# Down and output projections by token, with rows of the weights moving

## Chip, cores, metric

The kernel runs on one core of a Trainium2 chip. The metric is the time of one execution on the device, in microseconds (us).

## What is computed

A trunk of two layers over 256 tokens with 1024 channels, all in float32. Each layer is a gated ffn, a mixer and a second ffn; a norm stands ahead of each and behind the last.

```
def reference(x, ...):
    for l in range(L):
        h = rms_norm(x, ffn1_norm[l])
        x = x + 0.5 * swiglu_ffn(h, w_gate, w_up, w_down)   # 1024 -> 2816 -> 1024
        h = rms_norm(x, mix_norm[l])
        a_val, a_gate, b_u, b_v, c_b, c_c, c_x = split(h @ w_in[l])   # 1024 -> 2432
        a = a_val * sigmoid(a_gate)
        a = causal_depthwise_conv(a, conv_a_w[l]) + conv_a_b[l]       # 31 taps
        a = silu(layer_norm(a, ln_a_g[l], ln_a_b[l]))
        b = chunked_spatial_gating(gelu(b_u), gelu(b_v), ...)
        c = c_b * causal_depthwise_conv(c_c * c_x, conv_c_w[l])       # 3 taps
        x = x + concat(a, b, c) @ w_out[l]                            # 1024 -> 1024
        h = rms_norm(x, ffn2_norm[l])
        x = x + 0.5 * swiglu_ffn(h, ...)
    return rms_norm(x, final_norm)
```

## The kernel before, in words

The residual `x_sb` lies by channel: 8 tiles `x[d]` of 128 channels by 256 tokens. Weights come as float32 pages of 128x1024 (`load_to`, L114, six buffers). `split_to` (L121) divides a page into a high part `hi`, a cast on ACT (L128), and a low part `lo`, a difference on VectorE (L129), up to 14 pages ahead of their use. Activations are split in the same way and lie side by side as [high, low], 512 columns. `mm` (L170) is the product that fills nearly all of the time: a block of the high weights stands in the array and 512 columns move (L175), then the block of the low weights and 256 columns (L176). Here the two are called a pair. `whole` (L178) adds the two halves of the result with a copy on ACT and a sum on VectorE. Where float32 is used without a split, `mm_native` (L147) gives native products, which run as two instructions each; in the profile all of them have line L149.

An ffn (L349) goes through 22 hidden tiles in two halves of 11. For each tile it has 8 pairs for gate (`f_pg`) and 8 for up (`f_pu`); the results are multiplied on VectorE and ACT and split (`f_m`). Then the down projection of the half follows, `f_pd`, 8 output tiles of 11 pairs, each added to `x[d]`. In the second half `Norm.feed` (L297) makes the next stage's activations from each `x[d]` at once: scaled by the norm's gain and split. The norm's factor, which depends on the token alone, is applied later, to the results. Its sums over the channels are products with a column of ones (`token_sums`, L266), its inverse root a chain of small steps on VectorE (`rsqrt_rows`, L236), and it is spread to all partitions by products of 128x128 with an identity (L260). The first tile of the first ffn is native, because no page is split yet.

The mixer (L463 on) has 19 output tiles of 8 pairs in the combined projection (`m_p`). Group A runs a convolution over VectorE and ACT and then a layer norm (`m_la`, L412), on which the last three inputs of the output projection depend. Five of the eight output tiles of the output projection (`m_po`) are native, three in pairs. First come the inputs of groups B and C, and behind the layer norm those of A. The last step is the final norm and the multiply of `x_sb` by it (L669).

Order of work: each engine runs its instructions in a fixed order, which a scheduler derives from the program; where `pin` is used the program's own order stays.

Of the kernel before, what the change touches and what calls it, by code (L numbers as in the profile page):

```python
# [44 lines left out]
NCOLS = L * LCOLS + DT  # L45
# [7 lines left out]
IN_ORDER += [t for i in range(NC) for t in (C_C + i, C_X + i, C_B + i)]  # L53

PAGE_BLOCKS = 8
PAGE = PAGE_BLOCKS * P
RAWS = 6
PARTS = 15
LOAD_AHEAD = 6
AHEAD = 14  # L60
PACE = 1.6
NEXT = 4
# [14 lines left out]
def hybrid_trunk(ctx, tc, x_t, par, w_st, b_s, wts, out):  # L77
# [7 lines left out]
    ps_mm = ctx.enter_context(tc.tile_pool(name="ps_mm", bufs=6, space=PSUM))  # L85
    ps_sm = ctx.enter_context(tc.tile_pool(name="ps_sm", bufs=2, space=PSUM))

    spare = []

    def single(name):  # L90

        if not spare:
            pair = work.tile([P, 2, T], F32, tag="w", name=f"{name}_2")
            spare.extend([pair[:, 1, :], pair[:, 0, :]])
        return spare.pop()

# [14 lines left out]
    state = {"at": 0, "cap": None, "credit": 0.0}  # L111
# [20 lines left out]
    def native(n):  # L132

        at = state["at"]
        state["at"] += n
        last = (at + n - 1) // PAGE_BLOCKS
        load_to(last + LOAD_AHEAD)
        got = []
        for i in range(at, at + n):
            raw = loaded[i // PAGE_BLOCKS]  # L140
            c = i % PAGE_BLOCKS * P
            got.append(raw[:, c:c + P])
        while len(pages) <= last:
            pages.append(None)
        return got

    def mm_native(ps, w, act, ks, first, last):  # L147
        for k in ks:
            nc.tensor.matmul(ps, w[k], act[k], start=k == first, stop=k == last)  # L149

    def weights(n, ahead=True):
# [3 lines left out]
        last = (at + n - 1) // PAGE_BLOCKS  # L155
        split_to(last + 1)
        if ahead:
            state["credit"] += n * PACE / PAGE_BLOCKS
            to = min(last + 1 + AHEAD, len(pages) + int(state["credit"]))
# [3 lines left out]
        got = []  # L163
        for i in range(at, at + n):
            hi, lo = pages[i // PAGE_BLOCKS]
            c = i % PAGE_BLOCKS * P
            got.append((hi[:, c:c + P], lo[:, c:c + P]))
        return got

    def mm(ps, w, act, ks, first, last):  # L170


        for k in ks:
            (wh, wl), x2 = w[k], act[k]
            nc.tensor.matmul(ps, wh, x2, start=k == first, stop=False)  # L175
            nc.tensor.matmul(ps[:, 0, :], wl, x2[:, 0, :], start=False, stop=k == last)  # L176
# [11 lines left out]

    ones_sq = const.tile([P, P], F32, name="ones_sq")
    nc.vector.memset(ones_sq, 1.0)  # L190

    ps = ps_sm.tile([P, P], F32, tag="sm", name="warm")
    for _ in range(WARM):
        nc.tensor.matmul(ps, ones_sq, ones_sq, start=True, stop=True)
    x_sb = acts.tile([P, DT, T], F32, tag="x", name="x_sb")
    x = [x_sb[:, d, :] for d in range(DT)]
    xall = x_t.rearrange("p (d t) -> p d t", t=T)
    par_sb = const.tile([P, NCOLS], F32, name="par_sb")
    nc.sync.dma_start(par_sb, par)
    for i in range(2):  # L200
        raw = raws.tile([P, PAGE], F32, tag="raw", name=f"raw{i}")
        loaded.append(raw)
    Q, H = DT // 4, PAGE // 2
    for n, (i, h) in enumerate(((0, 0), (1, 0), (0, 1), (1, 1))):
        nc.sync.dma_start(x_sb[:, n * Q:(n + 1) * Q, :], xall[:, n * Q:(n + 1) * Q, :])
        nc.sync.dma_start(loaded[i][:, h * H:(h + 1) * H], wts[i][:, h * H:(h + 1) * H])
    ident = const.tile([P, P], F32, name="ident")
# [20 lines left out]
    def col(l, name, i):  # L228
        c = (L * LCOLS if name == "final_norm" else l * LCOLS + COL[name]) + i
# [501 lines left out]
```

## Time and profile before

| | |
|---|---|
| median of 3 runs | 962.69 us (960.36 to 965.59) |
| profiled execution | 961.55 us |
| its span, mean clock of TensorE | 959.8 us, 0.985 |
| PE (TensorE, products) | 934.6 us busy, 97% |
| PEld (its weight loads, beside PE) | 812.6 us, 85% |
| DVE (VectorE) | 776.9 us, 81% |
| ACT (ScalarE) | 568.7 us, 59% |
| DMA | 170.70 MB, 178 GB/s in the mean |

A span is the time from the first to the last instruction of one profiled execution. Shares are busy time over the span; clock is the share of full speed that TensorE had. Engines wait for each other by semaphores, and a wait is put down to what came last.

### The profile page before, as it was taken

The numbers are of one execution on the slowest core, as the hardware profiler recorded it, in microseconds if no ns is written. First come the engines' busy times: TensorE is split into PE (matmuls) and PEld (weight loads), VectorE is DVE, ScalarE is ACT, GpSimd is POOL, SyncE is SP. The second block draws the span as 40 slices with busy tenths as digits, with TensorE's granted clock in tenths as the row PEclk, the third lists the DMA queues.
The fourth block names the chain that finished last, engine by engine and source line by source line (L and its number), as shares of the span: only waits on it lengthen the run. The fifth ranks groups of instructions, "written<-read, shape, count | busy, mean of one in ns | idle before, by whom it ended". The sixth has DMA issues, their size and how long they took to land.

```text
span 959.8 us, 14578 instructions
## 1 busy us (share of the span) xinstructions
PE 934.6 (97%) x5280; PEld 812.6 (85%) x5280; DVE 776.9 (81%) x1456; ACT 568.7 (59%) x1052; POOL 3.0 (0%) x14
## 2 busy tenths in 40 slices
PE   9999999999979999999999999999997999999995
PEld 7888888888868888888888888888886888888885
DVE  6998777878969997777987777778987799878733
ACT  6875555578257864555655545556952677645522
POOL 0000000000000000000000000000000000000000
PEclk9999999999979999999999999999998999999998
DMA  8995555530037975555555555554300789555101
GB/s 297 320 347 192 185 194 188 186 133 22 17 114 261 340 272 184 190 195 181 189 181 186 187 190 186 195 184 145 111 1 0 245 284 341 196 188 194 45 1 44
DMA packets 48024, 170.70 MB, mean 178 GB/s; under 512 B 5328, under 2 KB 5712, under 8 KB 47952
## 3 DMA queue, kind: packets, MB, share of 16 engines
q1 hardware_dynamic: 47952, 169.77, 50.8%
q8 instruction: 41, 0.67, 0.3%
q14 instruction: 31, 0.25, 0.1%
HBM read 168.71 MB, written 1.05 MB: 177 GB/s over the span
## 4 chain that ended last, share of the span: by engine, by line
PE 91%; DVE 6%; DMA 2%; ACT 1%; issue 0%; DVEq 0%; SPq 0%
PE f_pd L175 17%; PE f_pu L175 17%; PE f_pg L175 17%; PE f_pd L176 9%; PE f_pu L176 8%; PE f_pg L176 8%; PE m_p L175 7%; PE m_p L176 4%; PE m_po L149 1%; DMA raw<-wts 1%; DVE m_ac_acc L458 1%; DVE lo L129 1%; DVE m_ac_acc L451 1%; PE f_pg L149 1%; DMA x_sb<-x_t 0%
## 5 line engine op out<-in xcount | busy, mean ns | idle before, releaser
L129 DVE TENSOR_TENSOR lo<-raw,hi 128x1024 fp32r<-128x1024 f32 x306 | 371.8, 1222 | 95.3 <-ACT hi L128 93.8
L128 ACT CAST hi<-raw 128x1024 fp32r<-128x1024 f32 x306 | 318.8, 1051 | 212.8 <-PE f_pd L175 71.6
L175 PE MATMUL f_pg<-ffn_norm_x,hi 128*128 128x512 f32 x696 | 247.4, 395 | 1.7 <-DVE ffn_norm_x L302 1.7
L175 PE MATMUL f_pd<-f_m,hi 128*128 128x512 f32 x704 | 247.2, 396 | 0.0
L175 PE MATMUL f_pu<-ffn_norm_x,hi 128*128 128x512 f32 x696 | 247.0, 394 | 0.0
L176 PE MATMUL f_pd<-f_m,lo 128*128 128x256 f32 x704 | 195.5, 280 | 0.0
L176 PE MATMUL f_pg<-ffn_norm_x,lo 128*128 128x256 f32 x696 | 194.4, 279 | 0.0
L176 PE MATMUL f_pu<-ffn_norm_x,lo 128*128 128x256 f32 x696 | 194.3, 279 | 0.0
L175 PEld LDWEIGHTS f_pd<-f_m,hi 128*128 128x128 f32 x704 | 131.9, 188 | 32.1 <-DVE f_m L334 1.4
L175 PEld LDWEIGHTS f_pg<-ffn_norm_x,hi 128*128 128x128 f32 x696 | 130.5, 187 | 32.3 <-DVE ffn_norm_x L302 2.3
L175 PEld LDWEIGHTS f_pu<-ffn_norm_x,hi 128*128 128x128 f32 x696 | 130.5, 187 | 30.0
L176 PEld LDWEIGHTS f_pd<-f_m,lo 128*128 128x128 f32 x704 | 132.8, 189 | 0.5
L176 PEld LDWEIGHTS f_pg<-ffn_norm_x,lo 128*128 128x128 f32 x696 | 131.2, 188 | 0.3 <-DVE lo L129 0.3
L176 PEld LDWEIGHTS f_pu<-ffn_norm_x,lo 128*128 128x128 f32 x696 | 131.2, 188 | 0.1
L175 PE MATMUL m_p<-mix_norm_x,hi 128*128 128x512 f32 x304 | 108.1, 398 | 0.0
L176 PE MATMUL m_p<-mix_norm_x,lo 128*128 128x256 f32 x304 | 85.9, 283 | 0.0
L175 PEld LDWEIGHTS m_p<-mix_norm_x,hi 128*128 128x128 f32 x304 | 57.1, 188 | 12.9
L176 PEld LDWEIGHTS m_p<-mix_norm_x,lo 128*128 128x128 f32 x304 | 57.4, 189 | 0.4 <-issue 0.2
L389 ACT ACTIVATE f_sg<-f_g 128x256 f32<-128x256 f32 x88 | 36.4, 414 | 17.5 <-DVE f_g L387 17.3
L185 DVE TENSOR_TENSOR f_wd_sm<-f_pd,f_wd_lo 128x256 f32<-128x256 f32 x64 | 26.8, 419 | 20.6 <-ACT f_wd_lo L183 20.6
L333 ACT CAST f_m<-f_m 128x256 fp32r<-128x256 f32 x88 | 35.4, 402 | 10.5 <-DVE f_m L391 7.2
L458 DVE SCALAR_TENSOR_TENSOR m_ac_acc<-apad,par_sb,m_ac_acc 128x256 f32<-128x256 f32 x90 | 40.8, 481 | 0.8 <-ACT m_ac_acc L446 0.7
(242 smaller groups left out, 843.2 us busy)
## 6 DMA issues: line engine op xcount, KB each, us to landing
raw<-wts SPq DMA_DIRECT2D x316, 512.0 KB, 4.3
x_sb<-x_t SPq DMA_DIRECT2D x4, 256.0 KB, 5.2
raw<-wts SPq DMA_DIRECT2D x4, 256.0 KB, 5.4
out<-x_sb SPq DMA_DIRECT2D x4, 256.0 KB, 2.4
wst<-w_st SPq DMA_DIRECT2D x2, 256.0 KB, 4.3
bsb<-b_s SPq DMA_DIRECT2D x2, 128.0 KB, 4.2
par_sb<-par SPq DMA_DIRECT2D x1, 143.0 KB, 2.3
```

Source lines behind the costliest of these rows:

```text
L128: nc.scalar.copy(hi, loaded[i])
L129: after(nc.vector.tensor_sub(lo, loaded[i], hi), held[0])
L149: nc.tensor.matmul(ps, w[k], act[k], start=k == first, stop=k == last)
L175: nc.tensor.matmul(ps, wh, x2, start=k == first, stop=False)
L176: nc.tensor.matmul(ps[:, 0, :], wl, x2[:, 0, :], start=False, stop=k == last)
L185: nc.vector.tensor_add(sm, ps[:, 0, :], lo)
L333: nc.scalar.copy(x2[:, 0, :], src)
L389: nc.scalar.activation(sg, g, AF.Silu)
L451: nc.vector.tensor_add(acc, acc, t)
L458: yield lambda j=j: nc.vector.scalar_tensor_tensor(acc[:, j % 4, :], ap[:, j:j + T], wt[j], acc[:, j % 4, :], ALU.mult, ALU.add)
```

## The change

The down and the output projection are turned round. The activation, a half of 128 tokens, stands in the array, and a row of a weight page moves, 512 columns at a time. The result lies by token. It takes three products (`mm_out`) for each token half c and column half h, and the four results (c, h) take four banks of PSUM that stay open through the whole stage. So the down projection of hidden tile f - 2 follows gate and up of tile f; the last three tiles are done bank by bank. `x_sb` lies by token as well: `x[c, h]`, 128 tokens by 512 channels. For the next norm each x must be turned back, by transposes on TensorE (`Norm.turn`), and the sum of squares comes from ACT as it squares (`accum_out`). The combined projection uses three products of 256 columns into one bank half, and no `whole`. In the output projection five inputs are split, all banks at once, and the three of group A are native, bank by bank. Buffers for raw pages go from 6 to 5, PSUM is 3 + 1 + 4 banks where it was 6 + 2, and pages are split up to 11 ahead, not 14. The pages of the weights are laid out in another order on the host, and x comes in two layouts.

```
+    def mm_three(ps, page, act, ks):
+        for k in ks:
+            (wh, wl), x2 = block(page, k), act[k]
+            nc.tensor.matmul(ps, wh, x2[:, 0, :], start=k == 0, stop=False)
+            nc.tensor.matmul(ps, wh, x2[:, 1, :], start=False, stop=False)
+            nc.tensor.matmul(ps, wl, x2[:, 0, :], start=False, stop=k == DT - 1)
+    def mm_out(ps, x2, page, c, h, first, last):
+        t, n = slice(c * P, (c + 1) * P), slice(h * N, (h + 1) * N)
+        if len(x2.shape) == 2:
+            nc.tensor.matmul(ps, x2[:, t], page[:, n], start=first, stop=last)
+            return
+        xh, xl = x2[:, 0, t], x2[:, 1, t]
+        wh, wl = (p[:, n] for p in page)
+        nc.tensor.matmul(ps, xh, wh, start=first, stop=False)
+        nc.tensor.matmul(ps, xh, wl, start=False, stop=False)
+        nc.tensor.matmul(ps, xl, wh, start=False, stop=last)
...
 class Norm:
+        def sums(self):
+            sq = [parts.tile([P, 4, T], F32, tag="pg", name=f"{self.id}_sq{i}") for i in range(2)]
+            for s, t in zip(sq, xt):
+                nc.scalar.activation(s, t, AF.Square)
+            s = sq[0]
+            nc.vector.tensor_add(s, s, sq[1])
+            nc.vector.tensor_add(s[:, :2, :], s[:, :2, :], s[:, 2:, :])
+            nc.vector.tensor_add(s[:, 0, :], s[:, 0, :], s[:, 1, :])
+            self.rs = rsqrt(token_sums([s[:, 0, :]], self.id), 1.0 / D, RMS_EPS, self.id)
+        def square(self, c, h):
+            sq = tmp.tile([P, N], F32, tag="sq", name=f"{self.id}_sq{c}{h}")
+            nc.scalar.activation(sq, x[c, h], AF.Square, accum_out=self.ss[:, c, h:h + 1])
+        def turn(self, c, h):
+            pt = small([P, 4, P], f"{self.id}_pt{c}{h}")
+            for d in range(4):
+                pin(nc.tensor.transpose(pt[:, d, :], x[c, h][:, d * P:(d + 1) * P], ident))
+            xg = tmp.tile([P, 4, P], F32, tag="xg", name=f"{self.id}_xg{c}{h}")
+            g = col(self.l, self.name, 4 * h, 4).rearrange("p (d o) -> p d o", o=1)
+            nc.vector.tensor_mul(xg, pt, g.broadcast_to([P, 4, P]))
+            hi, lo = (self.x2[h][:, :, i, c * P:(c + 1) * P] for i in range(2))
+            nc.scalar.copy(hi, xg)
+            nc.vector.tensor_sub(lo, xg, hi)
+        def lead(self, tiles, want):
+            ks = range(DT // 2), range(DT // 2, DT)
+            got = None
+            for mm, ps, w in tiles:
+                mm(ps, w, self.act, ks[0])
+                while self.later:
+                    self.later.pop(0)()
+            for mm, ps, w in tiles:
+                mm(ps, w, self.act, ks[1])
+                if got is None:
+                    got = self.rows(want)
+            return got
+    def drain_banks(order, bank, scale, nxt):
+        for n, (c, h) in enumerate(order):
+            ps = bank(c, h)
+            if n:
+                nxt.turn(*order[n - 1])
+            if scale is None:
+                nc.vector.tensor_add(x[c, h], ps, x[c, h])
+            else:
+                nc.vector.scalar_tensor_tensor(
+                    x[c, h], ps, scale[:, c:c + 1], x[c, h], ALU.mult, ALU.add)
+            nxt.square(c, h)
+        nxt.rstd()
+        nxt.later.append(lambda: nxt.turn(*order[-1]))
...
 def ffn(l, s, norm, nxt):
...
+            split_to(4)
+            norm.sums()
+            tiles[1] = [psum(wide, f"{nm}_1_pg")]
+            w1 = weights(2, False)
+            mm_wide(tiles[1][0], w1[0], act, range(DT))
+            rb, = norm.rows([AF.Copy])
...
+            if LAG <= f < FT - LAST + LAG:
+                for b in banks:
+                    down(f - LAG, *b)
+        def bank(c, h):
+            for f in range(FT - LAST, FT):
+                down(f, c, h)
+            return pd[c, h]
+        nxt.open()
+        if nxt.end:
+            finish(bank, rh, nxt)
+        else:
+            drain_banks(banks, bank, rh, nxt)
+    def finish(bank, scale, nxt):
+        for c in range(TC):
+            gx = []
+            for h in range(2):
+                ps = bank(c, h)
+                nc.vector.scalar_tensor_tensor(
+                    x[c, h], ps, scale[:, c:c + 1], x[c, h], ALU.mult, ALU.add)
+                nxt.square(c, h)
+                y = tmp.tile([P, N], F32, tag="xg", name=f"y{c}{h}")
+                nc.vector.tensor_mul(y, x[c, h], gfin[0][:, h * N:(h + 1) * N])
+                gx.append(y)
+            s = tmp.tile([P, 1], F32, tag="fin_s", name=f"fin_s{c}")
+            nc.vector.tensor_add(s, nxt.ss[:, c, 0:1], nxt.ss[:, c, 1:2])
+            r = rsqrt(s, 1.0 / D, RMS_EPS, f"fin{c}", 1)
+            for h, y in enumerate(gx):
...
+                nc.sync.dma_start(out[c, :, h * N:(h + 1) * N], y)
...
 def mixer(l, norm, nxt):
...
+        for k in OUT_ORDER[:DT - NA]:
+            w = weights(1, False)[0]
+            for c, h in banks:
+                mm_out(po[c, h], mix[k], w, c, h, k == first, k == last)
+        wn = dict(zip(OUT_ORDER[DT - NA:], native(NA)))
...
+        def bank(c, h):
+            for k in OUT_ORDER[DT - NA:]:
+                mm_out(po[c, h], mix[k], wn[k], c, h, k == first, k == last)
+            return po[c, h]
+        nxt.open()
+        drain_banks(banks, bank, None, nxt)
```

`mm_wide` is the old pair under a new name, pinned to the program's order.

**The start, TensorE.** Before, behind the native products of the first tile (`f_0`) the first pairs of the second tile follow, then the token sums (`ffn_norm_ps`):

```order
L149 MATMUL f_0_pu<-ffn_norm_xg_2_142,raw_94 128x256
L149 MATMUL f_0_pu<-ffn_norm_xg_2_151,raw_94 128x256 x2
L175 MATMUL f_1_pg<-ffn_norm_x_126,hi_190 128x512 [waits Activation_49]
L176 MATMUL f_1_pg<-ffn_norm_x_126,lo_191 128x256 [waits DVE_49]
L175 MATMUL f_1_pg<-ffn_norm_x_130,hi_190 128x512
L270 MATMUL ffn_norm_ps<-ones,ffn_norm_sq_200 128x1 [waits DVE_49]
L270 MATMUL ffn_norm_ps<-ones,ffn_norm_sq_200 128x1
```

In the change, where the natives have line L183 and pairs L191 and L192:

```order
L183 MATMUL f_0_pu<-ffn_norm_xg_2_146,raw_98 128x256
L183 MATMUL f_0_pu<-ffn_norm_xg_2_153,raw_98 128x256 x2
L309 MATMUL ffn_norm_ps<-ones,ffn_norm_sq_198 128x1 [waits DVE_49,PE_49]
L309 MATMUL ffn_norm_ps<-ones,ffn_norm_sq_198 128x1
L191 MATMUL f_1_pg<-ffn_norm_x_129,hi_188 128x512 [waits Activation_49]
L192 MATMUL f_1_pg<-ffn_norm_x_129,lo_189 128x256
```

The token sums now stand ahead of the first pair.

**Border from the first ffn to mixer 0, VectorE in the change.** L407 adds the four banks of the down projection (`f_pd`) to x, L365 multiplies a transposed bank (`mix_norm_pt`) by the gain, L368 is its low part, L276 to L287 are the inverse root, L152 is the low part of a page.

```order
L407 SCALAR_TENSOR_TENSOR x_sb<-f_pd_386,f_rh,x_sb 128x512 [waits PE_49]
L407 SCALAR_TENSOR_TENSOR x_sb<-f_pd_390,f_rh,x_sb 128x512 [waits PE_49]
L365 TENSOR_TENSOR mix_norm_xg_2021<-mix_norm_pt_2016,par_sb 128x512 [waits PE_49]
L407 SCALAR_TENSOR_TENSOR x_sb<-f_pd_394,f_rh,x_sb 128x512 [waits PE_49]
L368 TENSOR_TENSOR mix_norm_x_1974<-mix_norm_xg_2021,mix_norm_x_1974 128x4x128 [waits Activation_49]
L365 TENSOR_TENSOR mix_norm_xg_2042<-mix_norm_pt_2037,par_sb 128x512 [waits PE_49]
L407 SCALAR_TENSOR_TENSOR x_sb<-f_pd_398,f_rh,x_sb 128x512 [waits PE_49]
L368 TENSOR_TENSOR mix_norm_x_1974<-mix_norm_xg_2042,mix_norm_x_1974 128x4x128 [waits Activation_49]
L365 TENSOR_TENSOR mix_norm_xg_2063<-mix_norm_pt_2058,par_sb 128x512 [waits PE_49]
L372 TENSOR_TENSOR mix_norm_s<-mix_norm_ss 128x2 [waits Activation_49]
...
L287 SCALAR_TENSOR_TENSOR mix_norm_out<-mix_norm_r,mix_norm_y 128x2 [waits DVE_49]
L152 TENSOR_TENSOR lo_2198<-raw_1917,hi_2197 128x1024 [waits DMAHW0_49]
L368 TENSOR_TENSOR mix_norm_x_1975<-mix_norm_xg_2114,mix_norm_x_1975 128x4x128 [waits Activation_49]
```

The low part of the second bank stands behind the residual sum of the last; that of the last bank stands behind the inverse root and a page.

**Output projection of mixer 0, TensorE in the change.** L299 spreads the layer norm's factor, L206 are the native products of group A (`m_ao`) into the banks `m_po`, L362 transposes for the next norm.

```order
L299 MATMUL m_la_pb<-ident,m_la_out 128x128 [waits DVE_49]
L299 MATMUL m_la_pb<-ident,m_la_out 128x128
L206 MATMUL m_po_2988<-raw_2462,m_ao_2_2980 128x512 [waits DMAHW5_49,Activation_49]
L206 MATMUL m_po_2988<-raw_2500,m_ao_2_2983 128x512 [waits DMAHW6_49,Activation_49]
L206 MATMUL m_po_2988<-raw_2546,m_ao_2_2986 128x512 [waits DMAHW7_49,Activation_49]
L206 MATMUL m_po_2989<-raw_2462,m_ao_2_2980 128x512
L206 MATMUL m_po_2989<-raw_2500,m_ao_2_2983 128x512
L206 MATMUL m_po_2989<-raw_2546,m_ao_2_2986 128x512
L362 MATMUL ffn_norm_pt_3100<-ident,x_sb 128x128 [waits DVE_49]
L362 MATMUL ffn_norm_pt_3100<-ident,x_sb 128x128 x3
```

All 60 products of the split inputs stand ahead of these rows, two of them behind the layer norm's mean; the native ones follow bank by bank, and the transposes of a bank stand behind the products of the next.

## Rows read from the trace of the kernel before

**Rows 1.** The profile's page, part 1: engine, busy us (share of the span) xinstructions.

```profile
PE 934.6 (97%) x5280; PEld 812.6 (85%) x5280; DVE 776.9 (81%) x1456; ACT 568.7 (59%) x1052; POOL 3.0 (0%) x14
```

**Rows 2.** Timeline of PE in two stages: start us, duration us, engine, line, operation, out<-in, shape, count.

```profile
24.49 0.39 PE L175 MATMUL f_pu<-ffn_norm_x,hi 128*128 128x512 f32 x1
27.27 0.39 PE L175 MATMUL f_pg<-ffn_norm_x,hi 128*128 128x512 f32 x1
...
860.21 0.40 PE L175 MATMUL f_pg<-ffn_norm_x,hi 128*128 128x512 f32 x1
863.04 0.40 PE L175 MATMUL f_pu<-ffn_norm_x,hi 128*128 128x512 f32 x1
```

**Rows 3.** Stretches: length, busy us (xinstructions) of PE, PEld, DVE, ACT, POOL; clock, DMA share, GB/s.

```profile
274.00:280.00 6.00, 5.95 (x14) 4.80 (x15) 2.97 (x10) 3.65 (x8) 0.00 (x0) 0.51 0.18 59
305.00:445.00 140.00, 140.00 (x809) 123.40 (x808) 118.46 (x189) 89.09 (x153) 0.00 (x0) 1.00 0.69 235
830.00:945.00 115.00, 115.00 (x652) 99.64 (x651) 76.81 (x137) 53.71 (x100) 0.00 (x0) 1.00 0.30 105
```

**Rows 4.** Timeline of PE where two products of one kind stand side by side (a record may hold several).

```profile
77.16 0.62 PE L175 MATMUL f_pd<-f_m,hi 128*128 128x512 f32 x2
77.62 0.40 PE L176 MATMUL f_pd<-f_m,lo 128*128 128x256 f32 x2
77.86 0.40 PE L175 MATMUL f_pd<-f_m,hi 128*128 128x512 f32 x1
```

**Rows 5.** Groups by line and shape: down projection; busy us, mean ns, idle before.

```profile
L175 PE MATMUL f_pd<-f_m,hi 128*128 128x512 f32 x704 | 247.2, 396 | 0.0
```

**Rows 6.** Timeline of PE, mixer 0: the first native products to the next stage's first product.

```profile
254.19 0.59 PE L149 MATMUL m_po<-m_vt,raw 128*128 128x256 f32 x2
254.62 0.59 PE L149 MATMUL m_po<-m_bo,raw 128*128 128x256 f32 x2
...
266.27 0.70 PE L417 MATMUL m_la_mean<-m_ac,ones_sq 128*128 128x256 f32 x2 [0.74 <-DVE m_ac L461]
...
274.05 1.22 PE L149 MATMUL m_po<-m_ao,raw 128*128 128x256 f32 x2 [1.15 <-ACT m_ao L621]
...
291.96 0.40 PE L175 MATMUL f_pg<-ffn_norm_x,hi 128*128 128x512 f32 x1
```

**Rows 7.** Timeline of PE and DVE at the start.

```profile
13.33 1.89 PE L149 MATMUL f_pu<-ffn_norm_xg,raw 128*128 128x256 f32 x8
14.87 0.58 PE L175 MATMUL f_pg<-ffn_norm_x,hi 128*128 128x512 f32 x1
12.66 1.48 DVE L316 TENSOR_TENSOR ffn_norm_sq<-ffn_norm_sq,ffn_norm_sq 128x256 f32<-128x256 f32 x3
14.10 1.23 DVE L129 TENSOR_TENSOR lo<-raw,hi 128x1024 fp32r<-128x1024 f32 x1
```

**Rows 8.** Groups by line and shape: prices on ACT and DVE.

```profile
L128 ACT CAST hi<-raw 128x1024 fp32r<-128x1024 f32 x306 | 318.8, 1051 | 212.8 <-PE f_pd L175 71.6 <-PE f_pu L175 68.2 <-PE f_pg L175 67.8
L669 DVE TENSOR_TENSOR x_sb<-x_sb,final_norm_pb 128x512 f32<-128x512 f32 x4 | 2.5, 680 | 1.3 <-PE final_norm_pb L260 1.3
```

**Rows 9.** Chain that ended last, in order of time: start us, duration us, what.

```profile
203.75 0.44 PE mix_norm_pb L260 x4
...
483.31 0.34 PE ffn_norm_ps L270 x4
```

**Rows 10.** What PE waited for: us in total, times, longest us.

```profile
PE f_pg L175 <- DVE ffn_norm_x L302: 1.7, 2, 1.3
```

**Rows 11.** Timeline of ACT and DVE at the end of the span.

```profile
948.04 0.37 ACT L183 COPY f_wd_lo<-f_pd 128x256 f32<-128x256 f32 x1 [1.60 <-PE f_pd L176]
950.70 0.16 DVE L239 TENSOR_SCALAR final_norm_m<-final_norm_ps 128x2 f32<-128x2 f32 x1 [1.37 <-PE final_norm_ps L270]
...
952.41 0.16 DVE L250 SCALAR_TENSOR_TENSOR final_norm_y<-final_norm_r,final_norm_y 128x2 f32<-128x2 f32 x1
953.88 2.48 DVE L669 TENSOR_TENSOR x_sb<-x_sb,final_norm_pb 128x512 f32<-128x512 f32 x4 [1.31 <-PE final_norm_pb L260]
```

More of the change, by code (lines that the diff above doesn't have):

```diff
@@ L135, in native @@
         state["at"] += n
[L136 to L143, printed above, removed]
+        load_to(at + n - 1 + LOAD_AHEAD)
+        while len(pages) < at + n:
             pages.append(None)
[L145 to L149, printed above, removed]
+        return loaded[at:at + n]
     def weights(n, ahead=True):
@@ L255, in rsqrt_rows, with row @@
             y = y2
-        if between is not None:
-            between()
-        pb = ps_sm.tile([P, T], F32, tag="sm", name=f"{name}_pb")
-        for h in range(2):
+        return y
+    def row(y, name):
+        pb = small([P, T], f"{name}_pb")
+        for c in range(TC):
             pin(nc.tensor.matmul(
-                pb[:, h * P:(h + 1) * P], y[:, h:h + 1].broadcast_to([P, P]), ident,
+                pb[:, c * P:(c + 1) * P], y[:, c:c + 1].broadcast_to([P, P]), ident,
                 start=True, stop=True,
@@ new lines, in ffn, with down @@
+        tiles[1].append(ps_d.tile(wide, F32, tag="d00", name=f"{nm}_1_pu"))
+        mm_wide(tiles[1][1], w1[1], act, range(DT))
+        rh = tmp.tile([P, TC], F32, tag="rh", name=f"{nm}_rh")
+        nc.vector.tensor_scalar(rh, norm.rs, 0.5, None, ALU.mult)
+        mid, pd, wd = {}, {}, {}
+        def down(f, c, h):
+            if f not in wd:
+                wd[f] = weights(1)[0]
+            if (c, h) not in pd:
+                pd[c, h] = ps_d.tile([P, N], F32, tag=f"d{c}{h}", name=f"{nm}_pd{c}{h}")
+            mm_out(pd[c, h], mid[f], wd[f], c, h, f == 0, f == FT - 1)
@@ new lines, in ffn @@
+        for f in range(FT):
+            if f not in tiles:
+                w = weights(2)
+                tiles[f] = [psum(wide, f"{nm}_{f}_p{i}") for i in "gu"]
+                for ps, p in zip(tiles[f], w):
+                    mm_wide(ps, p, act, range(DT))
+            pg, pu = tiles[f]
+            g = tmp.tile([P, T], F32, tag="e", bufs=EVAC, name=f"{nm}_{f}_g")
+            nc.vector.tensor_mul(g, whole(pg, f"{nm}_{f}_wg"), rb)
+            sg = tmp.tile([P, T], F32, tag="e", bufs=EVAC, name=f"{nm}_{f}_sg")
+            nc.scalar.activation(sg, g, AF.Silu)
+            m = tmp.tile([P, T], F32, tag="e", bufs=EVAC, name=f"{nm}_{f}_m")
+            nc.vector.tensor_mul(m, whole(pu, f"{nm}_{f}_wu"), sg)
+            m2 = work.tile([P, 2, T], F32R, tag="w", name=f"{nm}_{f}_m2")
+            nc.scalar.copy(m2[:, 0, :], m)
+            nc.vector.tensor_sub(m2[:, 1, :], m, m2[:, 0, :])
+            mid[f] = m2
+            if f == FT // 2:
+                if s == 0:
+                    load_gating(l)
+                elif nxt.end:
+                    gfin.append(parts.tile([P, D], F32, tag="pg", name="gfin"))
+                    nc.sync.dma_start(gfin[0], gain)
+            if norm.first and f == 2:
+                for c in range(TC):
+                    nc.sync.dma_start(x_sb[:, c, :], x_n[c])
+            if LAG <= f < FT - LAST + LAG:
+                for b in banks:
+                    down(f - LAG, *b)
@@ L428, in layer_norm @@
                 between()
-        ps = token_sums(sq, name)
-        return xc, rsqrt_rows(
-            ps, 1.0 / (n * P), eps, name,
-            None if between is None else lambda: [between() for _ in range(more)])
+        y = rsqrt(token_sums(sq, name), 1.0 / (n * P), eps, name)
+        if between is not None:
+            for _ in range(more):
+                between()
+        return xc, row(y, name)
     def conv_ops(l, i, ap, out, name):
@@ L612, in mixer @@
             pass
+        for k in range(NA, DT):
+            split_mix(k)
         drain(len(back))
+        use([MM], [MM, SM])
         xc, pr = layer_norm(conv, LN_EPS, f"{nm}_la")
@@ L675, in _channels @@
+        ffn(l, 1, n2, norm)
 def _channels(a):
@@ L724 @@
     ]
[L725 removed]
+    out = nc.dram_tensor("out", (TC, P, D), F32, kind="ExternalOutput").ap()
     with tile.TileContext(nc) as tc:
```

402 lines of the change are left out of this document (162 added, 240 removed).

## The prediction, made blind

> **What bounds the kernel now.** I read the busy shares first. TensorE is busy for 934.6 of 959.8 us [rows 1], so the time is set by what TensorE streams, plus a few stops; VectorE, at 81%, matters only where TensorE waits for it. Next the timeline of TensorE, for the pitch of a pair (a 128x512 product and a 128x256 one, of one weight block). Eight pairs take 27.27 - 24.49 = 2.78 us in one place and 863.04 - 860.21 = 2.83 us in another [rows 2], thus 0.3475 and 0.354 us each. Both rhythms last: 809 products in 140 us are 0.346 us a pair, 652 in 115 us are 0.353 [rows 3]. I take 0.350 for the mean of the kernel. Where two products of one kind stand next to each other, two 512-column ones take 77.62 - 77.16 = 0.46 us and two of 256 columns 0.24 [rows 4]. So a 512-column product costs 0.232 and a 256-column one 0.118, whether its neighbour is of its kind or not. That is all there is for a price of the new streams: nothing in this trace runs a long row of 512s.
>
> The profiled execution took 961.55 us, 1.75 more than its span, and the median of three runs is 962.69 us. I make the sum against 961.55.
>
> **1. The streams.** The down projection has 704 pairs [rows 5], that is 8 for each of 88 hidden tiles (22 in 4 stages): 8 x 0.350 = 2.80 us a tile. Now a tile costs 12 products of 512 columns, 12 x 0.232 = 2.784 us. Over 88 tiles that gives -1.4 us. The combined projection has 304 pairs (19 output tiles, 8 inner tiles, 2 layers); each becomes three products of 256 columns, 0.354 for 0.350, +1.2 us. Gate and up are as before. The `whole` steps of both go, but ACT and VectorE do them beside TensorE, so I give them nothing. **-0.2 us.** For a low bound I take the native f32 products: one of 256 columns is two instructions and takes half of 254.62 - 254.19, 0.215 to 0.2165 an instruction [rows 6], nearly twice the 0.118 above; such an instruction thus streams what 512 columns stream, in a long row of its own kind, at 0.2165. That gives -18 us; the slow rhythm everywhere gives +10 us (both below, as rivals).
>
> By the Trainium skill (TensorE: Matmul & The Clock Gate, section Back-to-back issue gap), a matmul follows its neighbour after N/2.4 + 2.5 ns, 216 ns at 512 columns and 109 at 256. The pair would then be 0.325 us, and the rows have 0.3475 to 0.354, so the trace doesn't bear it out for these products. The same section gives some 131 ns for 512 columns in a long stream; no row here has one under 0.23.
>
> **2. The start.** Before, the first pair begins at 14.87, right behind the eight native products of f_pu; VectorE begins the low part of its page at 14.10, behind three sums of squares that begin at 12.66 [rows 7], and the token sums' products stand behind the second pair's first product. Now they are pinned ahead of the first pair, and they need much more: VectorE first does two low parts of pages (1.23 us each; I let them begin at about 13.2, in the middle of the three sums that are gone), ACT two squares of 128x1024 behind its two casts (I price a square as the cast of that size, 1.05 [rows 8]), then VectorE three sums of 1024, 512 and 256 columns (about 1.2, 0.7 and 0.4, in the proportion of [rows 7, 8]). Low parts and squares end at about 15.7, the sums near 18.0. TensorE goes on at about 18.2 instead of 14.87: **+3.3 us.** The low end is 0 (if the sums come early), the high end +5, when the stop also lowers the clock: after a comparable stop TensorE had 0.51 of its clock for 6 us [rows 3].
>
> **3. Transposes.** Each of the five borders between stages gets 16 transposes of 128x128. Four instructions of that size take 0.44 us [rows 9], so 16 x 0.11 = 1.76 us a border, 8.8 in all. At each border four products of token sums (0.34 us [rows 9]) go: -1.7. **+7.1 us.** All of it lies on TensorE, which has no slack. Bounds +5 and +9.
>
> **4. Waits at the borders.** Before, the first product of a stage needed one small step after the last tile; these waits sum to 1.7 us in the trace [rows 10]. Now, behind the last product of a stage VectorE has, in its order: the residual sum of the last bank, the low part of the second bank, the gain multiply and low part of the third, the rsqrt chain in between, the gain multiply of the fourth, the low part of a page, and the low part of the fourth. Six steps of 128x512 at 0.68 [rows 8], some 12 small ones at about 0.2 (eleven from 950.70 to 952.57 [rows 11]) and one page (1.23) make 7.7 us. TensorE has ahead of the product that needs the last one: eight transposes (0.9), three tiles with their first four inner tiles (12 x 0.35 = 4.2) and a few products more, 5.4 in all. So it waits 2.3 us at most by this count; the small steps fit in gaps where VectorE waits for a cast on ACT, and I take half of it, 1.2, for each of five borders: 6.0, less the 1.7 there are, **+4.3 us.** The low end is -1.7 (all hidden), the high one +12.
>
> **5. Output projection.** From the first native product of mixer 0, 254.19, to the first product of the next stage, 291.96, lie 37.8 us [rows 6]. Now 58 products of 512 columns stand ahead of the layer norm's mean (13.5 us). From the mean to the native products of group A stays a chain of 274.05 - 266.27 = 7.8 us [rows 6], which nothing covers in either version. Then 12 native products of 512 columns, each twice 0.433 us: 10.4. Before, the clock was at 0.51 from 274 to 280 [rows 3], half the work of 6 us lost; I keep 2.9 us for it. The sum is 34.6, which is 3.2 less, for two mixers **-6.5 us**; I trust it to 3 us either way. The mean can't come earlier than the convolution on VectorE, which ended its work at 266 before; 13.5 us put it at 267.7.
>
> **6. The end.** Last product to the end of the span takes 959.8 - 948.0 = 11.8 us now [rows 11]. In the change two token halves finish apart. After the last bank: residual sum 0.7, square on ACT about 0.6, a small sum 0.2, rsqrt 1.9, scaling 0.7, and 959.8 - 953.88 - 2.48 = 3.4 us from the last result to the end, 7.5. But the fourth product with the gain in this chain uses the buffer of an earlier result, which must have been written out, and in VectorE's queue it stands ahead of the last residual sum: about 1.8 more. 9.3 for 11.8, **-2.5 us** (from -4 to 0).
>
> Nothing is charged for the page loads: DMA's share is 0.69 and 0.30 in the long stretches [rows 3], and the loads after the output projection, for which two raw buffers are free, are asked for more than ten us ahead of use. If this cover were gone, each late page would cost up to 1.2 us of a split.
>
> The sum is -0.2 + 3.3 + 7.1 + 4.3 - 6.5 - 2.5 = +5.5: **967.0 us**, 0.45% above the median. About 0.5% is what a measurement of this kernel can tell from no change.
>
> **Rival A, faster.** Products of 512 columns in a row run at 0.2165 us. That is the pitch of the native instruction above, in long rows of one kind [rows 6]. There are 88 x 12 + 2 x 60 = 1176 of them; each saves 0.0155 us, 18.2 in all: about 949 us. For it: the pair mixes two kinds, and what it loses may be lost at the change of kind. Against: two neighbours of one kind take 0.46 us [rows 4]. The page named above gives the same figure. Chance 0.13.
>
> **Rival B, slower.** TensorE's rhythm is chosen anew at an interruption, and the change makes many more of them: 12 foreign products after every 16 pairs, and transposes. If it falls into the slow rhythm throughout, 1392 pairs of gate and up cost 0.354 instead of 0.350 (+5.3) and the 512s two thirds of 0.354, 0.236 (+4.7). That makes 977 us. Its place is the whole of the ffn stages; it decides where the pitch of gate and up is above 0.352 from the first stage on. For it: the last stage is slow for 115 us on end [rows 3]. Against: 140 us of stage three are fast. Chance 0.15.
>
> **Rival C, no change.** The waits at the borders are hidden, because the scheduler lets TensorE work on other tiles, and the start costs half: 967.0 - 4.3 - 1.7 = 961.0 us. For it: TensorE's first products of the next stage need only high parts. Against: the order of VectorE, which puts a page ahead of the last low part. Chance 0.22, of it 0.05 faster by over 0.5%.
>
> **How the numbers follow.** The forecast has 0.50, and its own range is 962 to 973; its middle lies just under the limit of 967.5, so 0.24 of it is "same" and 0.26 "slower". With C the same gets 0.41. Faster has 0.13 from A and 0.05 from C, 0.18; slower 0.26 and B's 0.15, 0.41. The range reaches from 952 (three quarters of A's gain and the waits as forecast) to 977 (B).
>
> **What would show it.** In the changed profile: 12 down products in 2.78 us; a first pair at about 18.2; four transposes in 0.44 us and 80 in all; waits of 1 to 2 us for VectorE or ACT at each border; 12 native products after an idle chain of about 8 us; some 9 us behind the last product. A pitch of 512s near 0.2165, or waits at the borders above 3 us each, would make the prediction wrong.

## The result and the profile after

The changed kernel takes **972.08 us** (971.86 to 972.51, 4 runs), the kernel before 961.81: a ratio of 1.0101, 95% interval 1.0071 to 1.0132. It is slower by 1%; 967.0 was forecast, within 952 to 977. The profiled execution took 972.09 us with a span of 970.4, 10.6 more than before.

Part 1 of the profile's page, answering to [rows 1]:

```profile
PE 941.5 (97%) x5192; PEld 803.7 (83%) x5192; DVE 703.9 (73%) x1202; ACT 534.7 (55%) x906; POOL 2.3 (0%) x14
```

TensorE still sets the time, though VectorE has 73 us less to do. Where the 10.6 us come from is read from the starts of products on TensorE in both traces:

| stretch | before | after | difference |
|---|---|---|---|
| start to the first pair | 14.87 | 19.71 | +4.8 |
| first pair to mixer 0 | 179.8 | 183.4 | +3.5 |
| mixer 0, first m_p to next f_pg | 97.3 | 96.7 | -0.6 |
| the two ffns between the mixers | 371.1 | 376.6 | +5.5 |
| mixer 1 | 97.0 | 97.8 | +0.8 |
| last ffn, to the start of its last product | 187.7 | 186.8 | -0.9 |
| from there to the end | 12.1 | 9.5 | -2.6 |

Timeline of PE at the start, answering to [rows 7]:

```profile
13.51 1.67 PE L183 MATMUL f_pu<-ffn_norm_xg,raw 128*128 128x256 f32 x7
...
19.28 0.58 PE L309 MATMUL ffn_norm_ps<-ones,ffn_norm_sq 128*128 128x1 f32 x4 [3.88 <-DVE ffn_norm_sq L351]
19.71 0.49 PE L191 MATMUL f_pg<-ffn_norm_x,hi 128*128 128x512 f32 x1
```

TensorE stands idle for 3.9 us, for the sums that are pinned ahead of the first pair. Behind this stop its clock falls. One stretch of the changed kernel, columns as in [rows 3]:

```profile
20.40:23.80 3.40, 3.40 (x13) 2.91 (x12) 3.19 (x12) 1.04 (x1) 0.00 (x0) 0.50 0.98 400
```

The granted clock is 0.50 for 3.4 us, so that the eight pairs of tile 1's gate take 4.44 us (19.71 to 24.15), where tile 2's take 2.77. The stop thus costs some 1.7 us more than the table's first line shows; they stand in its second. The kernel before has a clock of 1.00 from its first pair to its first mixer.

Next, what PE waited for, the rows that are new or answer to [rows 10]:

```profile
PE ffn_norm_ps L309 <- DVE ffn_norm_sq L351: 3.9, 1, 3.9
...
PE f_pd L210 <- DVE f_wu_sm L221: 2.2, 3, 0.9
...
PE f_pg L191 <- DVE ffn_norm_x L368: 1.4, 2, 1.0
...
PE m_p L199 <- DVE mix_norm_x L368: 0.8, 2, 0.4
```

The borders' own waits, 1.4 and 0.8, are small. The 2.2 us of `f_pd` stand elsewhere: the first down products of three stages are due before tile 0 is evaluated.

Timeline of PE, the first products of gate, up and down in one tile, and of the next gate:

```profile
103.99 0.39 PE L191 MATMUL f_pg<-ffn_norm_x,hi 128*128 128x512 f32 x1
...
106.80 0.40 PE L191 MATMUL f_pu<-ffn_norm_x,hi 128*128 128x512 f32 x1
...
109.63 0.40 PE L210 MATMUL f_pd<-hi,f_m 128*128 128x512 f32 x1
...
112.37 0.39 PE L191 MATMUL f_pg<-ffn_norm_x,hi 128*128 128x512 f32 x1
```

Eight pairs take 2.81 and 2.83 us, twelve down products 2.75, and so it stays: 76 of the gate tiles take 2.81, 78 of the up tiles 2.83, 72 of the down tiles 2.75. Of the two rhythms of [rows 2] gate and up have nearly the slow one throughout. Its form stands in the starts:

```profile
104.33 0.40 PE L191 MATMUL f_pg<-ffn_norm_x,hi 128*128 128x512 f32 x1
104.56 0.28 PE L192 MATMUL f_pg<-ffn_norm_x,lo 128*128 128x256 f32 x1
104.68 0.40 PE L191 MATMUL f_pg<-ffn_norm_x,hi 128*128 128x512 f32 x1
104.92 0.28 PE L192 MATMUL f_pg<-ffn_norm_x,lo 128*128 128x256 f32 x1
105.04 0.40 PE L191 MATMUL f_pg<-ffn_norm_x,hi 128*128 128x512 f32 x1
105.27 0.28 PE L192 MATMUL f_pg<-ffn_norm_x,lo 128*128 128x256 f32 x1
105.39 0.40 PE L191 MATMUL f_pg<-ffn_norm_x,hi 128*128 128x512 f32 x1
```

The 512s take 0.23, 0.24 and 0.23, and after three pairs, 1.06 us, it begins again (0.353 a pair); in the fast rhythm each pair is 0.23 and 0.117.

Below, "own time" is the sum of the distances from each product's start to the next start on TensorE. Without the waits gate and up have 493.5 us of it where they had 486.3 (the low clock's 1.7 is in it), the down projection 243.0 for 247.5, the combined projection 112.7 for 108.7.

### The profile page after: what moved, and what is told of

It reads as the page before. It is cut to its first block, busy times and chain, and to the rows that moved or that the text cites. A ratio compares the mean times of both kernels' runs of the same rounds, so it can differ in the third digit from the quotient of the medians.

```text
span 970.4 us, 13953 instructions
## 1 busy us (share of the span) xinstructions
PE 941.5 (97%) x5192; PEld 803.7 (83%) x5192; DVE 703.9 (73%) x1202; ACT 534.7 (55%) x906; POOL 2.3 (0%) x14
## 4 chain that ended last, share of the span: by engine, by line
PE 88%; DVE 5%; DMA 3%; ACT 2%; issue 1%; SPq 0%; DVEq 0%; ACTq 0%
PE f_pu L191 15%; PE f_pg L191 15%; PE f_pd L210 8%; PE f_pd L211 8%; PE f_pd L212 8%; PE f_pu L192 8%; PE f_pg L192 8%; PE m_p L199 4%; PE m_p L200 4%; PE m_p L198 4%; DMA raw<-wts 3%; PE m_po L206 2%; DVE lo L152 1%; PE m_po L210 1%; PE m_po L211 1%
## 5 line engine op out<-in xcount | busy, mean ns | idle before, releaser
L152 DVE TENSOR_TENSOR lo<-raw,hi 128x1024 fp32r<-128x1024 f32 x310 | 377.2, 1223 | 185.2 <-ACT hi L151 168.3
L151 ACT CAST hi<-raw 128x1024 fp32r<-128x1024 f32 x310 | 323.8, 1049 | 258.3 <-PE f_pg L191 88.8
L191 PE MATMUL f_pg<-ffn_norm_x,hi 128*128 128x512 f32 x696 | 250.8, 400 | 1.4 <-DVE ffn_norm_x L368 1.4
L191 PE MATMUL f_pu<-ffn_norm_x,hi 128*128 128x512 f32 x696 | 250.8, 400 | 0.0
L192 PE MATMUL f_pg<-ffn_norm_x,lo 128*128 128x256 f32 x696 | 195.9, 281 | 0.0
L192 PE MATMUL f_pu<-ffn_norm_x,lo 128*128 128x256 f32 x696 | 195.4, 281 | 0.0
L191 PEld LDWEIGHTS f_pg<-ffn_norm_x,hi 128*128 128x128 f32 x696 | 131.5, 189 | 34.0 <-DVE ffn_norm_x L368 2.6
L191 PEld LDWEIGHTS f_pu<-ffn_norm_x,hi 128*128 128x128 f32 x696 | 130.8, 188 | 32.2
L210 PE MATMUL f_pd<-hi,f_m 128*128 128x512 f32 x352 | 138.9, 395 | 2.2 <-DVE f_wu_sm L221 2.2
L211 PE MATMUL f_pd<-lo,f_m 128*128 128x512 f32 x352 | 138.3, 393 | 0.0
L212 PE MATMUL f_pd<-hi,f_m 128*128 128x512 f32 x352 | 136.5, 390 | 0.0
L192 PEld LDWEIGHTS f_pg<-ffn_norm_x,lo 128*128 128x128 f32 x696 | 132.0, 190 | 3.0
L192 PEld LDWEIGHTS f_pu<-ffn_norm_x,lo 128*128 128x128 f32 x696 | 131.6, 189 | 0.0
L199 PE MATMUL m_p<-mix_norm_x,hi 128*128 128x256 f32 x304 | 86.8, 287 | 0.8 <-DVE mix_norm_x L368 0.8
L198 PE MATMUL m_p<-mix_norm_x,hi 128*128 128x256 f32 x304 | 85.0, 286 | 0.0
L210 PEld LDWEIGHTS f_pd<-hi,f_m 128*128 128x128 f32 x352 | 66.1, 188 | 19.4 <-DVE f_wu_sm L221 3.4
L212 PEld LDWEIGHTS f_pd<-hi,f_m 128*128 128x128 f32 x352 | 66.0, 188 | 14.9 <-DVE f_m L467 0.7
L211 PEld LDWEIGHTS f_pd<-lo,f_m 128*128 128x128 f32 x352 | 66.1, 188 | 10.4
L199 PEld LDWEIGHTS m_p<-mix_norm_x,hi 128*128 128x128 f32 x304 | 58.2, 191 | 1.8 <-DVE mix_norm_x L368 1.2
L198 PEld LDWEIGHTS m_p<-mix_norm_x,hi 128*128 128x128 f32 x304 | 57.3, 191 | 0.2 <-issue 0.2
```

What stands on the lines that cost most here:

```text
L151: nc.scalar.copy(hi, loaded[i])
L152: after(nc.vector.tensor_sub(lo, loaded[i], hi), held[0])
L191: pin(nc.tensor.matmul(ps, wh, x2, start=k == 0, stop=False))
L192: pin(nc.tensor.matmul(ps[:, 0, :], wl, x2[:, 0, :], start=False, stop=k == DT - 1))
L198: nc.tensor.matmul(ps, wh, x2[:, 0, :], start=k == 0, stop=False)
L199: nc.tensor.matmul(ps, wh, x2[:, 1, :], start=False, stop=False)
```

## The experiments

Times are medians; ratios are against the kernel before on the same chip. That kernel itself has medians of 961.8 to 966.8 in the five measurements; the first of the two controls (c1) bears on why.

**First sums behind the first pairs** (e1): `sums` keeps the squares and their sums, and `root` has the token sums' products and the inverse root.

```
             norm.sums()
...
             mm_wide(tiles[1][0], w1[0], act, range(DT))
+            tiles[1].append(ps_d.tile(wide, F32, tag="d00", name=f"{nm}_1_pu"))
+            mm_wide(tiles[1][1], w1[1], act, range(DT // 2))
+            norm.root()
+            mm_wide(tiles[1][1], w1[1], act, range(DT // 2, DT))
             rb, = norm.rows([AF.Copy])
...
```

> The changed kernel with the products of the first token sums moved behind the first gate pairs and half of the up pairs of tile 1; nothing else. Theory (the pinned sums hold TensorE for about 4 us, 15.0 to 19.3): f_1_pg starts near 15.3, f_2_pg near 23 instead of 27.4, and the time falls by 4 to 4.5 us from 972.1 to about 967.8. Rival (the pages of tile 1 or the evaluation of tile 0 are as late as the sums): f_2_pg moves by less than 1 us, the time stays within 1 us of 972.1.

970.1 us (968.2 to 970.8), ratio 1.0070 (1.0043 to 1.0098): 2.0 us less than the changed kernel, half of what was expected. The profiled execution is the fastest of the four; its span is 966.5. There the first pair comes at 15.22, 4.5 us earlier, but tile 2 only 2.65 earlier (27.38 to 24.73):

```profile
24.73 0.50 PE L191 MATMUL f_pg<-ffn_norm_x,hi 128*128 128x512 f32 x1 [1.91 <-DVE f_g L468]
```

The clock stays at 1.00, and tile 1's gate takes 2.96 us instead of 4.44. A new wait of 1.9 us, and one of 0.6 for the norm's factor, take a part back: the banks for gate and up are all taken until tile 0 is evaluated. The theory holds for the wait, not for its whole price.

**Down projection three tiles behind** (e2): `LAG = 3` for `LAG = 2`.

> The changed kernel with the down projection three hidden tiles behind gate and up instead of two (the last three tiles bank by bank as before). Theory (at the start of a stage the factor of the norm comes late, so f_0 is not ready when its down products are due, three waits of 2.2 us in sum): these waits go and the time falls by about 2 us, to 970. Rival (what is late is the norm's factor itself, and TensorE runs out of free banks for gate and up instead): the wait moves to f_3_pg or f_2_pu and the time stays within 0.7 us of 972.1.

969.5 us (968.7 to 970.5), 1.0063 (1.0034 to 1.0093): 2.6 us less than the changed kernel. The `f_pd` waits are gone, and 0.7 us before f_pu (two waits, for banks) are new. The theory holds.

**Gate and up by kind** (e3).

```
         for k in ks:
-            (wh, wl), x2 = block(page, k), act[k]
-            pin(nc.tensor.matmul(ps, wh, x2, start=k == 0, stop=False))
-            pin(nc.tensor.matmul(ps[:, 0, :], wl, x2[:, 0, :], start=False, stop=k == DT - 1))
+            wh = block(page, k)[0]
+            pin(nc.tensor.matmul(ps, wh, act[k], start=k == 0, stop=False))
+        for k in ks:
+            wl = block(page, k)[1]
+            pin(nc.tensor.matmul(
+                ps[:, 0, :], wl, act[k][:, 0, :], start=False, stop=k == DT - 1))
```

> The changed kernel with the pairs of gate and up sorted by kind: the eight 512-column products of a tile first, then its eight 256-column products. Theory (a 512 behind a 512 takes 0.2267 and a 256 behind a 256 0.120, and the slow pattern of three pairs in 1.06 us belongs to the change of kind): a tile's 16 pairs take 16 x 0.347 = 5.55 us instead of 5.64, the time falls by 85 x 0.09 = 7 to 8 us, to about 964.5. Rival (the sum of one 512 and one 256 is the same whatever their order, 0.352): no change within 1 us.

965.5 us (963.2 to 967.2), 1.0021 (1.0005 to 1.0036). Timeline of PE, one tile:

```profile
103.59 1.98 PE L191 MATMUL f_pg<-ffn_norm_x,hi 128*128 128x512 f32 x8
105.41 1.11 PE L194 MATMUL f_pg<-ffn_norm_x,lo 128*128 128x256 f32 x8
106.36 2.00 PE L191 MATMUL f_pu<-ffn_norm_x,hi 128*128 128x512 f32 x8
108.20 1.00 PE L194 MATMUL f_pu<-ffn_norm_x,lo 128*128 128x256 f32 x7
```

Gate takes 2.77 us. Own time of gate and up falls by 6.3 us, the time by 6.6. The gain is there, a little under what was expected, since up takes 2.79.

**Combined projection in pairs** (e4): `mm_three` makes a 512- and a 256-column product, and `whole` stands behind each of the 19 tiles.

> The changed kernel with the combined projection back in pairs of 512 and 256 columns, with the copy on ACT and the sum on VectorE behind each tile. Theory (three 256-column products take 0.361 us in a row, a pair 0.347 to 0.354): TensorE's time in the two mixers falls by 304 x 0.007 to 0.014, 2 to 4.3 us, time 968 to 970. Rival (the copies and sums that come back hold the mixers up, as VectorE's convolution is what the output projection waits for): the gain comes back as a wait ahead of the layer norm's mean, time within 1 us of 972.1.

986.2 us (985.6 to 987.0), 1.0241 (1.0215 to 1.0268): **14 us worse**, which neither expected. On TensorE the pairs are cheaper, as the theory has it (own time without the waits 108.4 for 112.7). But from the first m_p to the layer norm's mean mixer 0 takes 81.9 us where the changed kernel takes 75.2. Stretches of both, changed kernel first (columns as in [rows 3]):

```profile
203.10:278.30 75.20, 74.68 (x565) 70.68 (x563) 68.54 (x146) 45.82 (x90) 0.64 (x1) 1.00 0.28 97
```
```profile
205.20:287.10 81.90, 77.38 (x413) 65.06 (x413) 74.27 (x163) 50.60 (x109) 0.88 (x1) 0.94 0.27 89
```

VectorE is busy for 91% of either. The 19 sums that come back cost it 7.9 us (0.417 each), and the mean comes 6.6 us later, in mixer 1 5.3: its products now wait for such a sum (`m_cwb_sm`, 2.9 us in both mixers together) and for the convolution (`m_ac`, 1.7), which share VectorE, and smaller waits stand ahead of them. The clock of 0.94 is part of the longer stretch; how much of it is not separated. In the changed kernel the `whole` steps, to which the prediction gave nothing, would set the pace of a mixer.

**The first three together** (e5).

> The changed kernel with the first sums moved behind the first pairs, the down projection three tiles behind, and gate and up sorted by kind, together. Theory (three separate losses, each on TensorE's path): their gains of 2 to 3.9, 2.6 and 6.5 us add up, 972.1 - 11 to 13 = 959 to 961, 1 to 4 us under the kernel before. Rival (the first two are one and the same wait at the start of the first stage, for the factor of the first norm): only the larger of them counts there, 963 to 964, no different from the kernel before.

963.4 us (961.3 to 964.3), 0.9966 (0.9944 to 0.9988): 8.7 us under the changed kernel, not 11 to 13. That is where the rival put it, and a part of the two losses is one: e1 alone already brings the waits of `f_pd` from 2.2 to 1.0 us. What remains are waits for banks (`f_pu` 2.2 us in three waits, `f_pg` 1.9), which the next run takes up.

**Two of the down banks lent to tile 2, with those three** (e8).

```
+                if f == 2:
+                    tiles[f] = [ps_d.tile(wide, F32, tag=t, name=f"{nm}_2_p{i}")
+                                for i, t in zip("gu", ("d10", "d01"))]
+                else:
+                    tiles[f] = [psum(wide, f"{nm}_{f}_p{i}") for i in "gu"]
```

> As the kernel with the three edits together, and gate and up of tile 2 take two of the four banks of the down projection, which are free until tile 3 is done. Theory (with three banks for gate and up TensorE waits at tile 2 until tile 0 has been evaluated: 1.9 us at the start, 0.7 at the borders): 2 to 2.6 us less than that kernel. Rival (tile 0's evaluation is late either way, and the wait moves to tile 3): within 0.7 us of it.

**958.3 us** (957.6 to 959.3), **0.9914** (0.9898 to 0.9930): 5.1 us less than with the three alone, and faster than either kernel. None of the waits of gate and up for banks is left; 1.0 us stands before down products instead. That it gains more than the 2 to 2.6 expected has a reason in the traces: timeline of PE at tile 2's gate, with the three alone, then with the lent banks.

```profile
25.21 3.61 PE L191 MATMUL f_pg<-ffn_norm_x,hi 128*128 128x512 f32 x8 [1.91 <-DVE f_g L471]
```
```profile
23.80 2.10 PE L191 MATMUL f_pg<-ffn_norm_x,hi 128*128 128x512 f32 x8
```

At the 1.9 us wait the granted clock of the first falls to 0.50 from 25.1 to 28.5; in the second it is 1.00 there. That makes 1.5 us besides the waits.

**Without transposes** (e6): `turn` multiplies x as it lies by the gain, without transposing.

> The changed kernel without the 80 transposes; the gain multiplies read x as it lies, so the activations of all stages but the first hold the wrong channels, while every other step stays. Theory (transposes cost their own 0.109 us each on TensorE and the borders' waits are separate): 8.7 us less, 963.4. Rival (transposes also break the products' row and hold back the low parts, so that a border costs more than its own transposes): 10 to 13 us less, 959 to 962.

962.7 us (960.0 to 964.1), 9.4 us less. This kernel leaves the transposes out and so computes something else. They cost about their own time, 80 x 0.109 us; the theory holds.

**The kernel before by kind** (e7): the same sorting in `mm`.

> The kernel before with all its pairs sorted by kind: the 512-column products of an output tile first, then its 256-column ones. Theory (both rhythms, 0.347 and 0.354, belong to alternating kinds; in rows of a kind a pair costs 0.227 + 0.120): 2400 pairs of 0.350 become 0.347, 7 us less than the kernel before, about 955. Rival (what the sorted order gains in the changed kernel comes from the neighbourhood of its 512-column down products): within 2 us of the kernel before.

960.9 us (959.8 to 961.8), 0.9940 (0.9924 to 0.9956) against 966.8 on that chip, but with a span of 960.1 no less than the first trace of the kernel before (959.8). A pair of gate and up has 0.350 us of own time, not 0.347: 80 gate and 80 up tiles take 2.79 us each, between the 2.77 and 2.83 of the two rhythms. Sorting makes the pitch steady, it doesn't make it fast; the time is 6 us above the expected 955.

**One different entry** (e9): in each gate or up tile the order is hi, hi, lo, lo, and then pairs.

```
+        turns = [(k, i) for k in ks for i in (0, 1)]
+        turns[1:3] = turns[2:0:-1]
+        for k, i in turns:
...
```

> The changed kernel with one pair in each gate or up tile entered differently: the 512-column products of the first two inner tiles first, then their 256-column ones, then pairs as before. Theory (the rhythm is set by how a row of pairs is entered): the pitch changes from 2.81 and 2.83 us a tile to 2.77, the time by up to 85 x 0.1 = 8 us, or the pattern of three pairs begins at another place. Rival (in rows that stand beside 512-column down products pairs always run in the slow rhythm): 2.81 to 2.83 us a tile as before, the time within 1 us of 972.1.

966.7 us (966.2 to 968.3), 1.0023 (1.0011 to 1.0036). Timeline of PE, starts of gate, up, down:

```profile
103.07 0.62 PE L195 MATMUL f_pg<-ffn_norm_x,hi 128*128 128x512 f32 x2
...
105.88 0.63 PE L195 MATMUL f_pu<-ffn_norm_x,hi 128*128 128x512 f32 x2
...
108.65 0.40 PE L215 MATMUL f_pd<-hi,f_m 128*128 128x512 f32 x1
```

Gate keeps 2.81, up takes 2.78 where it took 2.83, and down 2.73. The same products, with one place exchanged in each tile, save 5 us. That the entry acts on the rhythm is shown for up, and not for the gate, which was entered differently too; why the chip does it is open.

**Both kernels again** (c1, c2).

> The kernel before once more, unchanged, for a second trace of it. Theory (its time from run to run, 959 to 968 us, goes with how long its pairs stay in each of the two rhythms, 0.347 and 0.3535 a pair): the rhythms change at other places than in the first trace, and the own time of its 2400 pairs differs by as much as the span does. Rival (the runs differ in the start, in the DMAs): the rhythms change at the same places and the pairs take the same time to 1 us.

964.8 us (959.7 to 966.8, 10 runs), span 963.5. Timeline of PE in this second trace of the kernel before:

```profile
102.87 0.40 PE L175 MATMUL f_pg<-ffn_norm_x,hi 128*128 128x512 f32 x1
...
105.70 0.40 PE L175 MATMUL f_pu<-ffn_norm_x,hi 128*128 128x512 f32 x1
```

Eight pairs take 2.83 us here; the first trace has 2.77 in this place. The rows of pairs run fast up to 74 us in both traces, and then the first soon goes back to the fast rhythm, while the second stays slow to about 305. Own time of all pairs of the ffns and the combined projection is 5 us more, the span 3.7. So the difference of these two executions is the rhythm; that the spread of the others is so too is likely, but two traces don't show it.

> The changed kernel once more, unchanged, beside the kernel before on the same chip as the next run. Theory (its gate and up are always in the slow rhythm, since every tile enters them from 512-column products): 971.5 to 973 us, within 1 us of the first measurement, whatever the kernel before does on this chip. Rival (its time follows the chip as that of the kernel before does): a shift of 2 us or more.

971.6 us (971.1 to 973.2), 1.0079 (1.0054 to 1.0103) against 964.8. The changed kernel keeps its time to 0.5 us.

**Low parts on GpSimd** (e10): as e8, with `nc.gpsimd.tensor_sub` for the output projection's five split pages.

> As the kernel with the three edits and the extra banks, and the low parts of the output projection's five split pages made on GpSimd instead of VectorE, in both mixers; in TensorE's order the mean of the layer norm then stands behind 47 products of the output projection, not 59, and 13 products stand inside the layer norm's chain. Theory (from the first product of a mixer to the mean VectorE is the bound: 79 us of work in 75.5 us, 6.1 of them these low parts): the mean comes 3 to 6 us earlier in each mixer, a mixer takes 92 to 94 us instead of 97, the time falls from 958.3 to 950 to 953. Rival (TensorE's own products are the bound, or GpSimd is so slow, or so much in VectorE's way, that low parts come too late): a mixer takes 97 us or more and the time is 957 or above.

966.6 us (965.7 to 967.5), 1.0032 (1.0018 to 1.0045): 8 us worse than e8, as the rival had it. Timeline of DVE, then POOL, in mixer 0:

```profile
221.34 1.66 DVE L582 SCALAR_TENSOR_TENSOR m_ac_acc<-apad,par_sb,m_ac_acc 128x256 f32<-128x256 f32 x4
...
226.27 0.41 DVE L654 TENSOR_TENSOR m_bh<-m_p,mix_norm_rb 128x256 f32<-128x256 f32 x1
226.60 5.61 DVE L582 SCALAR_TENSOR_TENSOR m_ac_acc<-apad,par_sb,m_ac_acc 128x256 f32<-128x256 f32 x4
```
```profile
222.22 8.91 POOL L154 TENSOR_TENSOR lo<-raw,hi 128x1024 fp32r<-128x1024 f32 x3 [138.59 <-ACT hi L152]
```

Four steps of the convolution take 5.61 us beside GpSimd, where they took 1.66; the step that reads PSUM keeps its 0.41. Taken singly, two of the four take 2.30 and 2.60 and end at 228.90 and 231.42, each 0.28 us behind the end of a GpSimd step (228.62 and 231.14); the other two come after the last of the three and take 0.47. In the sum VectorE gains nothing: what is taken off it comes back as longer steps, and TensorE waits 9.7 us for the inner layer norm (`m_lv_pb`). The part of the theory on the chain was right: with products inside it, TensorE's 2 us before `m_la_pb` fall to 0.7. By the Trainium skill (SBUF — State Buffer, section SBUF: two separate sides) GpSimd and a VectorE step with two inputs in SBUF lock a shared pair of ports for a whole instruction. The two long steps agree with that; one such step at 222.53, inside the first GpSimd step, kept its 0.47.

## Why the prediction was right, and where it was off

The side and the range were right; the size was half, and "slower" had been given 0.41, no more than "same". By its own steps:

1. **Streams, -0.2 forecast: the step that failed.** It took gate and up "as before", at the mean of two rhythms. They cost 7.2 us more. About 1.7 of it is the low clock behind the stop at the start. The rest, 5.5, is the rhythm: behind a stage's first down products no tile is fast any more, 0.3525 us a pair. The five fast tiles of this trace (2.77) all stand ahead of those products, and so do the ten in the second trace (c2); e1 has two behind them. e3 and e9 show that order alone takes 5 to 7 us off. That the row of 512s sets the rhythm is what these traces suggest; e9 doesn't show it for the gate. The slow rhythm of gate and up is half of rival B (whose +5.3 is 5.6 by its own numbers). The other half didn't come: down products take 0.230, not 0.236, and save 4.5 us where 1.4 was forecast, in part because the old pairs had taken 0.352 there, not 0.350. Rival A's 0.2165 was not reached; the best 512s in a row take 0.227. The combined projection cost 4.0 for 1.2: a 256 behind a 256 takes 0.120, and with what stands between them three take 0.371 for 0.358 a pair.
2. **Start, +3.3:** measured +4.8, the mechanism as written, with 3.9 of wait; 0.2 stands ahead of the native products already (13.51 for 13.33). The step's high case, that the stop lowers the clock, came true as well: with its 1.7 the start cost 6.5, more than the bound of 5.
3. **Transposes, +7.1:** 80 at 0.109 (7.7 without a wait among them, own time 8.85 with it), less 1.7 of token sums: about 6.0 to 7.0. Right, and e6 confirms it.
4. **Waits at borders, +4.3:** 1.4 + 0.8 in the list of waits, and 1.2 around the last transposes of one border, 3.4 for the 6.0 forecast; less the old 1.7 that is +1.7. But 2.2 us that the sum hadn't, ahead of the first down products, fill the place. The sum came out nearly right for a wrong reason.
5. **Output projection, -6.5:** from the first product of mixer 0's output projection to the next stage 35.0 us for 37.8, in mixer 1 36.3 for 38.4: -4.9, with transposes in it that step 3 counts, so about -7.5 on the step's own terms. Right. Yet a mixer as a whole gained nothing, because the mean's last products come 3.7 us later after its start (75.2 us for 71.6). TensorE's own products make that up, from the same two steps: the combined projection 57.0 us for 54.7, and 58 products of the output projection 13.6 for the 50 native ones' 12.1. VectorE is done at the same moment (timeline of PE, then DVE):

```profile
278.29 0.70 PE L521 MATMUL m_la_mean<-m_ac,ones_sq 128*128 128x256 f32 x2
```
```profile
277.81 0.43 DVE L566 TENSOR_TENSOR m_ac<-m_ac_acc 128x256 f32<-128x256 f32 x1
```

Ahead of the mean VectorE lost the `whole` sums (8.3 us) and got eight more page splits (13 for 5, 9.7 us): fewer pages are split ahead, and five of the output projection instead of three are split at all. So both engines bound this stretch: in e6, without transposes, the mean's first products come 2.1 us sooner after the start of mixer 0 than in the changed kernel, its last ones 0.2. The prediction took VectorE's old end, 266, for its bound, and didn't price what the change adds there.
6. **End, -2.5:** measured -2.6. The size is right, one term of it is luck: no product with the gain stands ahead of the last residual sum, which begins at 961.74, 0.9 behind the start of its product. Two of them stand in the last inverse root instead (from 964.63 and 965.37 on), where they take 1.2 us of the chain.

Added up, the measured terms are 11.3 us (streams 6.7 with the low clock, start 4.8, transposes 6.0, borders 1.7, first down products 2.2, output projection -7.5, end -2.6) for the 10.6 between the spans, so no large term is missing.

Rival C's hidden borders came true in part, its smaller price of the start did not.

## What to carry to other kernels

A pitch read from a mix of products holds for that mix in that order; before a stream is rearranged, ask of each row which of its rhythms the new entry will bring, and sort products by kind where steadiness is wanted. Where an engine is busy for nine tenths of one stage, price what the change adds and takes there from that stage, splits and prefetch depth included, not from its mean share. And a product that is pinned ahead of a stream holds the whole stream until its inputs are there, as a bank does that is not yet free; the stop can cost clock behind it as well.

## Not expected of the hardware

Alternating 512- and 256-column products run in two rhythms, 0.347 and 0.353 us a pair, and keep one for 100 us or more. A single exchanged place moves it, and the same kernel differs in it from run to run. A GpSimd difference of 128x1024 takes 2.8 us in the mean here, and a VectorE step with two SBUF inputs that meets one can last until it ends (2.30 and 2.60 us instead of 0.47), while one that reads PSUM keeps its 0.41.
